# Fourteen pairs of gate tiles instead of twelve, with sums formed during attention, a result parked in DRAM, and low parts of ten weights made by transfers

## The chip, the cores and the metric

The kernel runs on one core of one Trainium2 chip. The metric is the time of one execution on the device in microseconds (us), the median of several runs. A profile is one execution recorded by the hardware profiler; its times are in us from the start of its span.

Engines are called as the profile calls them: PE (TensorE, the matmuls), PEld (PE's weight loads), DVE (VectorE), ACT (ScalarE), POOL (GpSimd), and SP (SyncE, whose queue issues most transfers; POOL's own queue issues the others).

## The reference

One layer of a backbone over 640 tokens (512 of a sample, 128 of a prompt) with 1024 features. An input `h` (a modulated norm of `x`) goes through four mixers, whose outputs are gated, summed, projected and added to `x`; a feed-forward part with a convolution follows. What bears on the change is this part:

```python
proj = h @ w_in                       # split into a_x a_b a_c b_q b_ff b_fb b_i b_g c_q c_k c_v d_u d_v
y_a = a_b * dwconv3(a_c * a_x, conv_a_w, conv_a_b)
y_b = hgrn2_bidir(b_q, b_ff, b_fb, b_i, b_g, ...)
y_c = neighbourhood_attention(c_q, c_k, c_v, ...)     # the prompt: context_attention
y_d = chunk_gmlp(d_u, d_v, ...)
g_a, g_b, g_c, g_d = split(sigmoid(h @ w_gate + b_gate), 4)
merged = g_a * (y_a @ w_br_a) + g_b * (y_b @ w_br_b) + g_c * (y_c @ w_br_c) + g_d * (y_d @ w_br_d)
x = x + g1 * (merged @ w_o)
```

`w_gate` is 1024 x 4096, each `w_br` 256 x 1024, each y 640 x 256.

## The kernel before

**Precision.** Every large product is made of three matmuls on numbers split in two. A weight `raw` (F32) is copied by ScalarE into a high part (F32R), and the low part is `raw - high`, a subtraction on VectorE; `feat` (L356) loads a weight tile and does both, `split_y` (L682) does it for a branch's y, `g_split` (L1058) for an operand of `h`. For some weights of the feed-forward part the low part is made without VectorE: `low_dma` (L1370) has ScalarE write `-high` into the place of the low part, and then POOL's queue sends `raw` there by a transfer that adds (`accum_op=ALU.add`). With `xh` and `xl`, high and low part of `h`, a product is `wh*xh + wh*xl + wl*xh`.

**Tiles.** A tile is 128 output features by 640 tokens, in two halves of 320 (`HC`), so a matmul is 128 x 128 by 320 columns. `gemm` (L392) does 3 matmuls for each of the 8 blocks of 128 input features and each half: 48. A plain gate tile (`gate_tile`, L980) makes these 48 for `h @ w_gate`, takes a sigmoid on ScalarE, makes 12 more for `y @ w_br`, and VectorE multiplies the two and adds them to `merged` (regions MG0, MG1): 60 matmuls.

**Pairs.** Two gate tiles n and n + 4 of one branch are also computed together: input features, output features and tokens cut in halves make a 2 x 2 by 2 x 2 block product, which takes 7 block products instead of 8 (`gprod`, L1128, numbered 1 to 7, of 12 matmuls each). For this, sums of weight blocks are formed for each pair (`g_sums`, `g_b`, `g_c`) and four sums of blocks of `h` once for all (`g_operands`, L1029). With a11, a12, a21, a22 for the blocks of h (first index the half of the features or of the tokens as the code has it): a22 := a21 - a22, a21 := a11 - a21, a11 := a22 - a11, a12 := a12 + a11; the last is operand 3, the others operands 5, 7 and 6. Each is then split into high and low part.

A pair is written out by hand in `g_pair` (L1166): in one call stand the products of pair p, the end of pair p - 1 (its second sigmoid, branch and merge), and the preparation of the weights of pair p + 1. Instructions made through `ovec`, `oact` and `opool` keep their order in the program there. `gp_load` (L1066) loads a pair's two raw weights (10 blocks of 128 x 128 each, 640 KB), one into the rotating pool `raw` (3 buffers), the other into `raw` or region G by turns; the prepared weights go into the pool `w` (3 buffers) for even pairs and into regions C, B, D for odd ones (`gunit`, L1075). The first pair's weights are prepared by `g_first` (L1214) ahead of the last plain gate tiles.

**Order of stages.** A list `units` holds projections in the order of `SECTIONS` (last: ck, cq, cv, ac, ax, ab, two tiles each), then the plain gate tiles, then the pairs. `ahead` loads a unit's weight up to 4 units ahead and prepares it up to 2 ahead. The order of the branches is d, a, b, c (`BR`); before, the eight tiles of branch d are plain and a, b, c are done as 12 pairs (`PAIRS`). Jobs that run beside them are Python generators that are advanced by `tick`, whose argument counts the matmul time issued: `hgrn` gives y_b, `gmlp` y_d, `conva` y_a, `attn` y_c, `ada_cols` the modulation's columns (`w_adt`, loaded into A and H). The order of instructions on each engine's queue thus follows from these yields and from the scheduler, and `drain` advances the jobs until something is done.

**Places.** Regions (A to H, X0, X1, F, MG0, MG1, XH, XL0, XL1, S0) are named pieces of on-chip memory; a new use of a region waits for the last use of the old one. C holds y_c and B attention's operands; E holds the split y_b and D the split y_d; `h` in F32 was written to DRAM at the start (`hdr`). `attn` (L738) has, for each of 16 units, `s1` (scores, exponential), `s2` (normalisation on VectorE, transposes on PE) and `s3` (product with the values). y_c is written to DRAM (`ycd`) after attention and is read back into A by POOL's queue when the last pair of branch b is through (L1180).

The lines that say where the sums stand before:

```python
        if (bi, n) == (0, 0):
            start(g_operands())
    ...
    def g_operands():
        while "yc" not in R:
            yield 1
        nc.sync.dma_start(ycd, R["yc"].bitcast(F32))
        f = [region(t, [P, 2, 4, HC]) for t in "CB"]
```

Of the kernel before, what the change touches and what calls it, by code (L numbers as in the profile page):

```python
# [16 lines left out]
P = 128  # L17
# [3 lines left out]
BRIDGE = 4  # L21
LORD = "w0 1 5 w1 w2 2 6 3 7"
SPL = 0
WARM = [80, 120]
UE = [5, 3]
XP = ()
XE = ()
T = 640
# [22 lines left out]
def tile_step(ctx: ExitStack, tc: tile.TileContext, a: dict, outs: list, dbg=None):  # L51
# [301 lines left out]
        act(w[0], raw, AF.Copy)  # L353
        vec.tensor_tensor(w[1], raw, w[0].bitcast(F32), ALU.subtract)  # L354

    def feat(src, kt=8):  # L356

        raw = rp.tile([P, kt, P], F32, tag="raw", name=nm("raw"))
        nc.sync.dma_start(raw, src)

        def prep(parts=False, tag=None):
            if tag is None:
                w = wp.tile([P, 2, kt, P], F32R, tag="w", name=nm("w"))
            else:
                w = region(tag, [P, 2, kt, P], F32R)
            act(w[:, 0], raw, AF.Copy)  # L366
            low = lambda: vec.tensor_tensor(w[:, 1], raw, w[:, 0].bitcast(F32), ALU.subtract)  # L367
            if parts:
                return w, low
            low()  # L370
            return w
        return prep
# [52 lines left out]
    def evac_in(sec, n, ps):  # L425
        psv = None if isinstance(ps, list) else ps[:, :, 0:HC]
        if sec in ("ff", "fb"):
            d = 0 if sec == "ff" else 1
            ff = need("A", "FF", [P, 2, 2, T])
            kk = need("B", "KK", [P, 2, 2, T])  # L430
            if psv is None:
                for c in range(2):
                    cs = slice(c * HC, (c + 1) * HC)
                    act(ff[:, d, n, cs], ps[c], AF.Sigmoid)
                    act(kk[:, d, n, cs], ps[c], AF.Sigmoid, scale=-1.0)
            else:
                act(c2(ff[:, d, n]), psv, AF.Sigmoid)
                act(c2(kk[:, d, n]), psv, AF.Sigmoid, scale=-1.0)
            i = d * 2 + n
            vec.tensor_scalar(ff[:, d, n], ff[:, d, n], oml[:, i:i + 1], lb[:, i:i + 1],  # L440
                              ALU.mult, ALU.add)
            vec.tensor_scalar(kk[:, d, n], kk[:, d, n], oml[:, i:i + 1], None, ALU.mult)
        elif sec == "q":
            dd = need("D", "HD", [P, 2560])
            act(c2(dd[:, n * T:(n + 1) * T]), psv, AF.Silu)
        elif sec == "g":
            o = need("MG1", "HO", [P, 2560])
            act(c2(o[:, 1280 + n * T:1280 + (n + 1) * T]), psv, AF.Silu)
        elif sec == "du":
            x0 = need("X0", "DX0", [P, 2560])  # L450
            act(c2(x0[:, n * T:(n + 1) * T]), psv, AF.Copy)
        elif sec in ("ac", "ax", "ab"):
            if (sec, n) == ("ac", 0):
                drain(lambda: "hgrn_out" in R)
            y = need("MG0", "YA", [P, 2, 2, T])
            if sec == "ac":
                act(c2(y[:, 0, n]), psv, AF.Copy)
                return
            if sec == "ab":
                drain(lambda: "conv" in R)  # L460
            x = y[:, 0 if sec == "ax" else 1, n]
            vec.tensor_tensor(c2(x), psv, c2(x), ALU.mult)  # L462
            if (sec, n) == ("ab", 1):
                drain(lambda: "ada39" in R)
                R["ya"] = split_y("A", y[:, 1].rearrange("p n t -> p (n t)"))
        elif sec in ("ck", "cq", "cv"):
            if sec == "cv":
                dst = need("G", "CG", [P, 1280])[:, n * T:(n + 1) * T]
            else:
                f = need("F", "CF", [P, 2560])  # L470
                o = 0 if sec == "ck" else 1280
                dst = f[:, o + n * T:o + (n + 1) * T]
            sc = 0.125 if sec == "cq" else 1.0
            cg, cw = (4, 16) if sec == "cq" else (8, 8)
            dv = dst[:, 0:TS].rearrange("p (g r c) -> p r g c", g=cg, r=8)
            for (b, r0, r1) in ((0, 0, 5), (1, 5, 8)):
                src = ps[:, b, 0:(r1 - r0) * 64].rearrange("p (r g c) -> p r g c", g=cg, c=cw)
                act(dv[:, r0:r1], src, AF.Copy, scale=sc)
            act(dst[:, TS:T], ps[:, 1, 192:320], AF.Copy, scale=sc)

    def hgrn():
# [184 lines left out]
        for t in range(5):  # L668
# [6 lines left out]
                vec.scalar_tensor_tensor(s, m[:, pr * P:(pr + 1) * P],  # L675
                                         p1[:, C_HN + pr:C_HN + pr + 1], s, ALU.mult, ALU.mult)
            yield 0.4
        R["yb"] = split_y("E", sg)
        R["hgrn_done"] = True
        R["yd"] = split_y("D", R["yt"])  # L680

    def split_y(tag, y):  # L682
        w = region(tag, [P, 2, 2, T], F32R)
# [54 lines left out]
    def attn():  # L738
# [46 lines left out]
        for pr in range(2):  # L785
            ten.transpose(m[:, pr * P:(pr + 1) * P], cv[:, pr * T + TS:(pr + 1) * T], ident)
            pe(0.11)
        vec.tensor_copy(vpt, m[:, 0:256])
        nc.sync.dma_start(o_cv[0, 0].rearrange("h s d -> s h d"), vpt.rearrange("p (h d) -> p h d", h=4))
        yield 0.4  # L790
        ast = sp.tile([P, 48], F32, tag="ast", name=nm("ast"), bufs=1)
# [106 lines left out]
        for u in range(0, 16, 2):  # L898
            if u < 14:
                s1(u + 2)  # L900
                yield HD[6]
            for i in range(2):
                s2(u + i)
                yield 1.2
            s3(u)
            yield HD[8]
        R["yc"] = yc

    ld, rd = {}, {}
# [8 lines left out]
    def in_tile(sec, n, w):  # L918
        ps = pg()
        gemm(ps, w, 0, 8, xhk, xlk)  # L920
        evac_in(sec, n, ps)
        if n == 1:
            R[sec + "_done"] = True
        if n == 1 and sec in starts:
            start(starts[sec](), 1.5, SLACK[sec])
            if sec == "q":
                start(ada_cols(range(16, 40), "S0", col_home, HD[4]), HD[7])

# [30 lines left out]
    for s in SECTIONS:  # L959
        for n in range(2):  # L960
# [1 line left out]
                plain(lambda s=s, n=n: rows(a["w_tok"][TOK.index(s), n], 4, 256),  # L962
                      lambda w, s=s, n=n: tok_tile(s, n, w))
            else:
                plain(lambda s=s, n=n: feat(a["w_in"][OFF[s] // P + n]),
                      lambda w, s=s, n=n: in_tile(s, n, w))

    hdr = dram.tile([2, P, 4, T], F32, name="hdr")
# [1 line left out]

    BR = ["d", "a", "b", "c"]
    GI = dict(a=0, b=1, c=2, d=3)
    PAIRS = [(bi, n) for bi in range(1, 4) for n in range(4)]
    GPAIR = len(PAIRS)
    ycd = dram.tile([P, 2, 2, T], F32, name="ycd")
    merged = []
    MHT = ["E", "A", "B", "D"]
    mh = []

    def gate_tile(bi, n, w):  # L980
        br = BR[bi]
        if (bi, n) == (0, 0):
            start(g_operands())
        ps = pg()
        gemm(ps, w, 0, 8, xhk, xlk)
        gt = gp.tile([P, T], F32, tag="gt", name=nm("gt"))
# [23 lines left out]
    for bi in range(4):  # L1010
        for n in range(8):
# [2 lines left out]
            br = BR[bi]  # L1014

            def ld_(bi=bi, n=n, br=br):
                return feat(a["w_gate"][GI[br] * 8 + n], 10)

            def cp(w, bi=bi, n=n):
                gate_tile(bi, n, w)  # L1020
# [6 lines left out]
    gx, gw = {}, {}  # L1027

    def g_operands():  # L1029
        while "yc" not in R:  # L1030
            yield 1
        nc.sync.dma_start(ycd, R["yc"].bitcast(F32))
        f = [region(t, [P, 2, 4, HC]) for t in "CB"]
        for c in range(2):
            for h in range(2):
                nc.sync.dma_start(f[c][:, h], hdr[h][:, :, c * HC:(c + 1) * HC])
        yield 8
        (a11, a12), (a21, a22) = [[x[:, h] for h in range(2)] for x in f]
        ops = {i: region(t, [P, 2, 4, HC], F32R) for i, t in ((6, "X0"), (5, "X1"), (7, "F"))}
        gx["x"] = {i: (x[:, 0], x[:, 1]) for i, x in ops.items()}  # L1040
        for i, h, c in ((1, 0, 0), (2, 1, 0), (4, 1, 1), (3, 0, 1)):
            cs = slice(c * HC, (c + 1) * HC)
            gx["x"][i] = xh[:, 4 * h:4 * h + 4, cs], xl[h][:, :, cs]
        gx["t3"] = a12
        vec.tensor_tensor(a22, a21, a22, ALU.subtract)
        yield 1.5
        vec.tensor_tensor(a21, a11, a21, ALU.subtract)
        yield 1.5
        vec.tensor_tensor(a11, a22, a11, ALU.subtract)
        yield 1.5  # L1050
        vec.tensor_tensor(a12, a12, a11, ALU.add)
        yield 1.5
        for i, x in ((6, a11), (5, a22), (7, a21)):
            g_split(i, x)
            yield 1.5
        R["gx"] = True

    def g_split(i, x):  # L1058
# [107 lines left out]
    def g_pair(p_, r):  # L1166
# [902 lines left out]
```

## Time and profile before

| | us |
|---|---|
| median of 3 runs | 1047.86 |
| lowest, highest | 1046.7, 1052.12 |
| the profiled execution's own time | 1051.51 |
| its span, first to last instruction | 1049.7 |
| PE busy | 1030.0 (98%) |
| VectorE busy | 795.3 (76%) |
| ScalarE busy | 518.7 (49%) |
| POOL busy | 95.6 (9%) |
| mean granted clock | 0.993 |

The page gives the span in 40 slices of some 26 us; this is PE, VectorE and the clock, in tenths:

```profile
PE   8999999999999999999999999999999999999997
DVE  6558789789967377677768688998888887695734
PEclk9999999999999999999999999999999999999999
```

In a row of instructions the first numbers are the start and the duration (timeline) or the busy time and the mean duration in ns (groups), then engine, line, operation, `output<-input` with the program's names, sizes, and in brackets the idle time ahead and what ended it. Matmuls overlap: the duration of one is longer than the step from one to the next. In the chain of waits a row is a stretch of the chain that ended last: start, length, engine and line. The releasers are worked out from semaphore events.

### The profile page before, as it was taken

The page shows a single profiled execution, that of the slowest core. Times are in us where ns is not written, and L with a number is a line of the kernel's source. Part 1 is how long each engine was busy: PE and PEld are TensorE (multiplying, and loading weights), DVE is VectorE, ACT ScalarE, POOL GpSimd, SP SyncE. Part 2 cuts the span into 40 slices and gives each one's busy share as a digit, 9 for nine tenths or more (in the row PEclk, how much of TensorE's full clock was granted, in tenths as well). Part 3 has the DMA queues.
Part 4 walks back from the last instruction along what each step waited for, and adds up shares of the span by engine and source line. Part 5 has one row for each costly group of instructions (what it writes and reads, how often), then busy time and mean ns, then how long its engine had stood idle before and what let it go on. Part 6 is the DMA issues. An engine that isn't in the chain of part 4 may idle for free.

```text
span 1049.7 us, 18767 instructions
## 1 busy us (share of the span) xinstructions
PE 1030.0 (98%) x7648; PEld 967.4 (92%) x7648; DVE 795.3 (76%) x1284; ACT 518.7 (49%) x889; POOL 95.6 (9%) x139
## 2 busy tenths in 40 slices
PE   8999999999999999999999999999999999999997
PEld 6799989999889999999998889999999998888886
DVE  6558789789967377677768688998888887695734
ACT  6252343333243345444445377777677775632532
POOL 1000010202100000000000011221111121000201
PEclk9999999999999999999999999999999999999999
DMA  9663433454234131431258475666665559974212
GB/s 372 238 246 119 135 96 119 125 177 150 70 117 148 53 117 55 147 99 55 89 203 319 159 256 132 171 162 163 162 161 152 146 151 262 340 264 161 81 41 101
DMA packets 52855, 165.67 MB, mean 158 GB/s; under 512 B 7808, under 2 KB 14880, under 8 KB 49696
## 3 DMA queue, kind: packets, MB, share of 16 engines
q1 hardware_dynamic: 42992, 137.19, 38.3%
q0 software_dynamic: 9776, 27.28, 11.1%
q8 instruction: 60, 0.98, 0.4%
q14 instruction: 27, 0.22, 0.1%
HBM read 131.52 MB, written 21.52 MB: 146 GB/s over the span
## 4 chain that ended last, share of the span: by engine, by line
PE 92%; DVE 2%; DMA 2%; issue 2%; ACT 1%; POOL 0%; SPq 0%; POOLq 0%; ACTq 0%; DVEq 0%
PE g L1476 19%; PE g L401 19%; PE m L1135 14%; PE g L1789 8%; PE m L1789 6%; PE m L1476 5%; PE g L1148 4%; PE m L1271 3%; PE g L947 2%; PE g L1271 2%; PE g L1891 1%; PE m L562 1%; PE m L211 1%; PE m L887 1%; DMA E<-actd 1%
## 5 line engine op out<-in xcount | busy, mean ns | idle before, releaser
L401 PE MATMUL g<-XH,w 128*128 128x320 f32 x832 | 201.2, 318 | 0.2 <-DVE MG L462 0.2
L401 PEld LDWEIGHTS g<-XH,w 128*128 128x128 f32 x832 | 143.1, 189 | 2.8 <-issue 2.0
L401 PE MATMUL g<-XL,w 128*128 128x320 f32 x416 | 129.6, 311 | 0.0
L401 PEld LDWEIGHTS g<-XL,w 128*128 128x128 f32 x416 | 78.9, 190 | 0.8 <-issue 0.5
L354 DVE TENSOR_TENSOR w<-raw,w 128x1024 fp32r<-128x1024 f32 x34 | 41.5, 1221 | 16.1 <-ACT w L353 15.3
L1789 PE MATMUL g<-w,XH 128*128 128x512 f32 (+1 forms) x216 | 47.5, 372 | 0.0
L353 ACT ACTIVATE w<-raw 128x1024 fp32r<-128x1024 f32 x34 | 35.8, 1053 | 19.1 <-PE g L1271 9.8
L1789 PEld LDWEIGHTS g<-w,XH 128*128 128x128 f32 x216 | 38.5, 188 | 7.3 <-DVE X L131 0.2
L1135 PE MATMUL m<-XH,w 128*128 128x320 f32 x192 | 45.0, 309 | 0.0
L366 ACT ACTIVATE w<-raw 128x1024 fp32r<-128x1024 f32 (+1 forms) x29 | 32.5, 1121 | 23.3 <-PE g L401 7.5
L367 DVE TENSOR_TENSOR w<-raw,w 128x1024 fp32r<-128x1024 f32 (+1 forms) x29 | 37.5, 1294 | 5.7 <-ACT w L366 5.5
L131 DVE SCALAR_TENSOR_TENSOR X<-MG,p2t,X 128x641 f32<-128x641 f32 x44 | 38.9, 884 | 2.2 <-ACT X L131 1.4
L1789 PE MATMUL m<-w,XH 128*128 128x512 f32 (+1 forms) x180 | 40.3, 369 | 0.0
L1789 PE MATMUL g<-w,XL 128*128 128x512 f32 (+1 forms) x180 | 40.1, 373 | 0.0
L131 DVE SCALAR_TENSOR_TENSOR X<-X,p2t,X 128x641 f32<-128x641 f32 x44 | 38.9, 884 | 1.2 <-ACT X L131 0.3
L1476 PE MATMUL g<-XL,C 128*128 128x320 f32 x240 | 38.6, 310 | 0.4 <-ACT MG L131 0.4
L1476 PE MATMUL g<-XL,w 128*128 128x320 f32 x240 | 38.7, 310 | 0.0
L1789 PEld LDWEIGHTS g<-w,XL 128*128 128x128 f32 x180 | 32.2, 188 | 6.8 <-DVE dt L1800 0.6
L1476 PEld LDWEIGHTS g<-XL,C 128*128 128x128 f32 x240 | 35.9, 188 | 1.1 <-ACT MG L131 1.1
L1476 PEld LDWEIGHTS g<-XL,w 128*128 128x128 f32 x240 | 35.9, 188 | 0.7 <-ACT MG L131 0.3
L1789 PEld LDWEIGHTS m<-w,XH 128*128 128x128 f32 x180 | 31.3, 189 | 5.3
L1789 PE MATMUL m<-w,XL 128*128 128x512 f32 (+1 forms) x150 | 33.2, 368 | 0.0
(544 smaller groups left out, 2703.9 us busy)
## 6 DMA issues: line engine op xcount, KB each, us to landing
raw<-in_w_up_dram SPq DMA_DIRECT2D x31, 512.0 KB, 5.1
raw<-in_w_gp_dram SPq DMA_DIRECT2D x18, 640.0 KB, 4.0
raw<-in_w_in_dram SPq DMA_DIRECT2D x22, 512.0 KB, 4.4
raw<-in_w_down_dram SPq DMA_DIRECT2D x22, 512.0 KB, 4.0
H<-in_w_adt_dram SPq DMA_DIRECT2D x16, 512.0 KB, 4.3
actd<-X POOLq DMA_DIRECT2D x22, 320.5 KB, 5.5
G<-in_w_up_dram SPq DMA_DIRECT2D x11, 512.0 KB, 4.7
X<-in_w_adt_dram SPq DMA_DIRECT2D x10, 512.0 KB, 3.7
```

Of the source, the lines that this page charges most:

```text
L131: r = f(*args, **kw)
L353: act(w[0], raw, AF.Copy)
L354: vec.tensor_tensor(w[1], raw, w[0].bitcast(F32), ALU.subtract)
L366: act(w[:, 0], raw, AF.Copy)
L367: low = lambda: vec.tensor_tensor(w[:, 1], raw, w[:, 0].bitcast(F32), ALU.subtract)
L401: mm(o, w[:, h, k0 + k, :], r(k)[:, s], start=(k == 0 and i == 0), stop=(k == kt - 1 and i == 2))
L947: mm(o, x(kx)[:, ts], w[:, h, k, :], start=(kx == 0 and i == 0), stop=(kx == 7 and i == 2))
L1135: mm(o, w[:, k, :], x[:, k, :], start=(first and k == 0 and j == 0), stop=(k == 3 and j == 2), skip_group_check=True)
L1148: mm(pb[:, c, 0:HC], w[:, h + k, :], y[:, x, k, s], start=(k == 0 and j == 0), stop=(k == 1 and j == 2))
L1271: mm(m, mh[k // 2][:, hx, k % 2, t * P:(t + 1) * P], wo[q][:, hw, k % 2, :], start=(k == 0 and i == 0), stop=(k == 7 and i == 2))
L1476: mm(o, w[:, k, :], x[:, k, :], start=(first and k == 0 and j == 0), stop=(k == 3 and j == 2), skip_group_check=True)
L1789: mm(acc[nh][t + c0 // 256][:, 0:c1 - c0], sl[k][hx][:, t * P:(t + 1) * P], w[:, hw, k, c0:c1], start=(kk_ == 0 and k == 0 and i == 0), st ...
```

## The change

- Two of the four pairs of branch d, (0,2) and (0,3), are done as pairs too: 14 pairs, and four plain gate tiles (n = 0, 1, 4, 5). `merged` of these is begun by `g_merge`.
- `g_operands` starts when the projection cv is through. Once attention has taken its copies of cv (`R["cg"]`) it loads three pieces of h from `hdr`, two into D and one into G, and makes three of the four sums as soon as y_a is there. It splits operand 7 into F when the last scores are done (`R["scores"]`), and operands 5 and 6 into X1 and X0 when attention is over. Then the fourth piece of h is loaded into D; it is added in the first pair.
- y_b is split into D and written to DRAM (`ybd`), so that D is free, and is read back into E by POOL's queue after pair (0,3). y_d is split into E.
- The weights of ac, ax, ab and of the four plain gate tiles, ten in all, get their low part by `low_dma`.
- `g_operands` holds G, so the first pair's second raw weight goes into the rotating pool and G is used for odd pairs. Odd pairs use the regions in the order B, C, D.
- The write of y_c to `ycd` moves to the end of `attn`.

```diff
+NPL = 2
+LOWD = ("ac", "ax", "ab", "d")
...
-    def feat(src, kt=8):
+    def feat(src, kt=8, dma=False):
...
             act(w[:, 0], raw, AF.Copy)
+            if dma:
+                low_dma(w[:, 1].rearrange("p a b -> p (a b)"), raw.rearrange("p a b -> p (a b)"))
+                return w
...
+    ybd, ycd = [dram.tile([P, 2, 2, T], F32, name=n) for n in ("ybd", "ycd")]
...
-        R["yb"] = split_y("E", sg)
+        nc.sync.dma_start(ybd, split_y("D", sg).bitcast(F32))
         R["hgrn_done"] = True
-        R["yd"] = split_y("D", R["yt"])
+        R["yd"] = split_y("E", R["yt"])
...
         vec.tensor_copy(vpt, m[:, 0:256])
+        R["cg"] = True
...
+            if u == 14:
+                R["scores"] = True
...
+        nc.sync.dma_start(ycd, yc.bitcast(F32))
         R["yc"] = yc
...
             start(starts[sec](), 1.5, SLACK[sec])
+            if sec == "cv":
+                start(g_operands())
...
-    PAIRS = [(bi, n) for bi in range(1, 4) for n in range(4)]
+    PAIRS = [(0, n) for n in range(NPL, 4)] + [(bi, n) for bi in range(1, 4) for n in range(4)]
...
-        if (bi, n) == (0, 0):
-            start(g_operands())
...
-                return feat(a["w_gate"][GI[br] * 8 + n], 10)
+                return feat(a["w_gate"][GI[br] * 8 + n], 10, br in LOWD)
...
     def g_operands():
-        while "yc" not in R:
+        while "cg" not in R:
             yield 1
-        nc.sync.dma_start(ycd, R["yc"].bitcast(F32))
-        f = [region(t, [P, 2, 4, HC]) for t in "CB"]
-        for c in range(2):
-            for h in range(2):
-                nc.sync.dma_start(f[c][:, h], hdr[h][:, :, c * HC:(c + 1) * HC])
-        yield 8
-        (a11, a12), (a21, a22) = [[x[:, h] for h in range(2)] for x in f]
-        ops = {i: region(t, [P, 2, 4, HC], F32R) for i, t in ((6, "X0"), (5, "X1"), (7, "F"))}
-        gx["x"] = {i: (x[:, 0], x[:, 1]) for i, x in ops.items()}
+        d, g = region("D", [P, 2, 4, HC]), region("G", [P, 4, HC])
+        part = lambda h, c: hdr[h][:, :, c * HC:(c + 1) * HC]
+        for x, h, c in ((d[:, 0], 0, 1), (d[:, 1], 1, 1), (g, 0, 0)):
+            nc.sync.dma_start(x, part(h, c))
+        while "ya" not in R:
+            yield 1
+        a21, a22, a11 = d[:, 0], d[:, 1], g
+        vec.tensor_tensor(a22, a21, a22, ALU.subtract)
+        yield 2
+        vec.tensor_tensor(a21, a11, a21, ALU.subtract)
+        yield 2
+        vec.tensor_tensor(a11, a22, a11, ALU.subtract)
+        gx["x"] = {}
         for i, h, c in ((1, 0, 0), (2, 1, 0), (4, 1, 1), (3, 0, 1)):
             cs = slice(c * HC, (c + 1) * HC)
             gx["x"][i] = xh[:, 4 * h:4 * h + 4, cs], xl[h][:, :, cs]
-        gx["t3"] = a12
...
-        for i, x in ((6, a11), (5, a22), (7, a21)):
+        for i, x, t, key in ((7, a21, "F", "scores"), (5, a22, "X1", "yc"), (6, a11, "X0", "yc")):
+            while key not in R:
+                yield 1
+            y = region(t, [P, 2, 4, HC], F32R)
+            gx["x"][i] = y[:, 0], y[:, 1]
             g_split(i, x)
             yield 1.5
+        nc.sync.dma_start(a22, part(1, 0))
+        gx["t3"] = a22, a11
         R["gx"] = True
...
-        r.append(region("G", [P, 10, P]) if p_ % 2 == 0 else rp.tile([P, 10, P], F32, tag="raw", name=nm("raw")))
+        r.append(region("G", [P, 10, P]) if p_ % 2 else rp.tile([P, 10, P], F32, tag="raw", name=nm("raw")))
...
-        return region("CBD"[i], [P, 5, 4, P], F32R)
+        return region("BCD"[i], [P, 5, 4, P], F32R)
...
-        ovec.tensor_tensor(c2(gt), pb, c2(gt), ALU.mult)
         mg = merged[n // 4][:, n % 4, :]
+        ovec.tensor_tensor(c2(gt if bi else mg), pb, c2(gt), ALU.mult)
+        if not bi:
+            return
         ovec.tensor_tensor(mg, mg, gt, ALU.add)
...
-            if PAIRS[q] == (1, 3):
-                R["yc"] = region("A", [P, 2, 2, T], F32R)
-                pool.dma_start(R["yc"], ycd)
+            if PAIRS[q] in ((0, 3), (1, 3)):
+                n_, t, y = ("yb", "E", ybd) if PAIRS[q][0] == 0 else ("yc", "A", ycd)
+                R[n_] = region(t, [P, 2, 2, T], F32R)
+                pool.dma_start(R[n_], y)
...
+        if q < 0:
+            t3, x6 = gx["t3"]
+            ovec.tensor_tensor(t3, t3, x6, ALU.add)
         if nx:
             g_a(n, r[n])
         gprod(b3, p_, 2, q < 0)
         if q < 0:
-            g_split(3, gx["t3"])
+            g_split(3, gx["t3"][0])
...
     def g_first(r):
+        drain(lambda: "ada39" in R)
         g_a(0, r[0])
```

More of the change, by code (lines that the diff above doesn't have):

```diff
@@ L964, in tile_step @@
             else:
-                plain(lambda s=s, n=n: feat(a["w_in"][OFF[s] // P + n]),
+                plain(lambda s=s, n=n: feat(a["w_in"][OFF[s] // P + n], dma=s in LOWD),
                       lambda w, s=s, n=n: in_tile(s, n, w))
@@ L972, in tile_step @@
     GI = dict(a=0, b=1, c=2, d=3)
-    PAIRS = [(bi, n) for bi in range(1, 4) for n in range(4)]
+    PAIRS = [(0, n) for n in range(NPL, 4)] + [(bi, n) for bi in range(1, 4) for n in range(4)]
     GPAIR = len(PAIRS)
-    ycd = dram.tile([P, 2, 2, T], F32, name="ycd")
     merged = []
@@ L1043, in g_operands @@
             gx["x"][i] = xh[:, 4 * h:4 * h + 4, cs], xl[h][:, :, cs]
-        gx["t3"] = a12
[L1045 to L1052, printed above, removed]
-        for i, x in ((6, a11), (5, a22), (7, a21)):
+        for i, x, t, key in ((7, a21, "F", "scores"), (5, a22, "X1", "yc"), (6, a11, "X0", "yc")):
[3 more added lines that the diff above has]
+            gx["x"][i] = y[:, 0], y[:, 1]
             g_split(i, x)
             yield 1.5
+        nc.sync.dma_start(a22, part(1, 0))
+        gx["t3"] = a22, a11
         R["gx"] = True
```

## The prediction

> **What bounds the kernel now.** I began with the page's spans and engine shares, then asked who TensorE (PE) waited for, and then how busy each engine is in the stages that the change touches: 207 to 307 us (attention beside the projections and the first gate tiles), 307 to 363 (the other gate tiles), and one pair (363 to 379).
>
> ```profile
> span 1049.7 us, 18767 instructions
> PE 1030.0 (98%) x7648; PEld 967.4 (92%) x7648; DVE 795.3 (76%) x1284; ACT 518.7 (49%) x889; POOL 95.6 (9%) x139
> ```
> ```profile
> PE g L1891 <- ACT XH L1853: 2.6, 2, 1.5
> ...
> PE g L401 <- DVE MG L462: 0.2, 1, 0.2
> ```
> ```profile
> 207.00:307.00 100.00, 99.62 (x715) 89.76 (x714) 86.63 (x180) 35.37 (x75) 12.41 (x16) 1.00 0.35 112
> 307.00:363.00 56.00, 56.00 (x384) 56.00 (x383) 27.05 (x26) 19.77 (x21) 0.00 (x0) 1.00 0.38 130
> 363.00:379.00 16.00, 16.00 (x111) 16.00 (x110) 12.75 (x20) 7.78 (x15) 0.00 (x0) 1.00 0.36 124
> ```
> The columns after the stretch and its length are PE, weight load, VectorE (DVE), ScalarE (ACT) and POOL busy, the granted clock, DMA share and GB/s. PE is busy 98% of the span, and from 207 to 379 it lacks 0.38 us. The longest wait, 2.6 us in two parts, lies in the opening; here the only one listed is 0.2 us. The clock is 1.00. So this part ends when PE has worked off its matmuls: only fewer matmuls shorten it, and each new wait of PE lengthens it by its full size. VectorE, 87% busy until 307, is the engine nearest behind.
>
> **What the change removes.** A pair takes 7 products of 12 matmuls and two branches of 12, 108; two plain tiles take 2 x 60 = 120. Two more pairs save 24 matmuls of 320 columns.
>
> ```profile
> 352.17 1.92 PE L401 MATMUL g<-D,w 128*128 128x320 f32 x12
> 353.93 0.31 PE L401 MATMUL g<-XH,w 128*128 128x320 f32 x1
> ```
> ```profile
> 306.53 56.37 PE g L401 x383
> 362.89 8.80 PE m L1135 x60
> ```
> The first fence is PE's timeline, the second the chain of waits. The single matmul of 0.31 us overlaps its neighbours: twelve take 353.93 - 352.17 = 1.76 us, 0.147 each. The chain says the same of a plain tile (56.37 / 383 = 0.147) and of a product (8.80 / 60 = 0.147). So the gain is 24 x 0.147 = **3.5 us** and no more; multiplying by 0.31 would give twice that.
>
> Ten weights lose their subtraction on VectorE and get a negated copy on ScalarE and an accumulating transfer from POOL's queue.
>
> ```profile
> L367 DVE TENSOR_TENSOR w<-raw,w 128x1024 fp32r<-128x1024 f32 (+1 forms) x10 | 13.2, 1324 | 0.5 <-ACT w L366 0.4
> ```
> ```profile
> 318.10 1.49 DVE L1045 TENSOR_TENSOR B<-B 128x1280 f32<-128x1280 f32 x1 [5.17 <-DMA B<-hdr]
> ```
> VectorE loses 13.2 us before 307 and gets there three sums of h and one low part of a sum, 4 x 1.49 = 6.0, and some 2 us of the first pair's weights: about 5 us less. ScalarE gets ten copies of about 1.2 us, 11.6, on 35.37 busy of 100. As sums of busy time these cost PE nothing, being hidden under the 99.62 us of matmuls. What can cost is the order in each queue, which I took from the two compiled programs.
>
> **Transfers moved.** The second branch's y goes to DRAM before three pieces of h may be loaded into the same place, so the sync queue waits for that write, and behind it stand a projection weight and a modulation column load.
>
> ```profile
> 219.44 1.49 DVE L686 TENSOR_TENSOR E<-MG,E 128x1280 fp32r<-128x1280 f32 x1 [1.34 <-ACT E L685]
> ```
> ```profile
> 231.31 0.35 SPq L244 DMA_DIRECT2D A<-in_w_adt_dram  x1
> ```
> ```profile
> raw<-in_w_gp_dram SPq DMA_DIRECT2D x18, 640.0 KB, 4.0
> G<-in_w_gp_dram SPq DMA_DIRECT2D x6, 640.0 KB, 3.9
> C<-raw POOLq DMA_DIRECT2D x10, 256.0 KB, 4.1
> ycd<-C SPq DMA_DIRECT2D x1, 1280.0 KB, 9.0
> B<-X POOLq DMA_DIRECT2D x1, 384.0 KB, 6.3
> ```
> y is split by 220.9; a write of this size landed after 9.0 us; 229.9 is ahead of 231.3, when the column load was issued anyway. Cost 0. The reloads of y by POOL (the third branch's was there before) are asked for a pair and more ahead of use: 0.
>
> **Attention's first transposes.** The changed program places them 13 matmuls (1.9 us) earlier in PE's order, with a sum of h (1.49) put ahead of their operand on VectorE and a subtraction (1.2) gone.
>
> ```profile
> 243.45 0.41 DVE L867 TENSOR_SCALAR X<-X,ast 128x384 f32<-128x384 f32 x1
> ```
> ```profile
> 244.73 0.49 PE L870 MATMUL m<-cst,X 128*128 128x128 f32 x3
> ```
> Here the operand was ready 0.9 us before PE came. PE now comes at 242.8 and finds it at 243.9 + 0.3 or a little later: a wait of 1.4 to 1.6 us if nothing gives. Later in attention VectorE has less to do, and PE gets part of it back; bounds 0 and 1.6, I take **0.4**, nearer the lower end because VectorE's load falls.
>
> **The first gate tile's sigmoid.** This is where I expect the main cost. The first pair's second raw weight is now loaded into a rotating buffer whose last user is the third gate weight, and that is free only when the weight's low-part transfer has landed. ScalarE's order then holds a copy of this raw weight *ahead* of attention's last exponentials and the first gate tile's sigmoid; the second tile's matmuls need the sigmoid's PSUM bank.
>
> ```profile
> 276.84 1.27 ACT L366 ACTIVATE w<-raw 128x1280 fp32r<-128x1280 f32 x1 [1.05 <-PE g L401]
> ...
> 284.10 1.27 ACT L685 ACTIVATE A<-MG 128x1280 fp32r<-128x1280 f32 x1
> ...
> 291.31 0.62 ACT L860 ACTIVATE X<-X,ast 128x384 f32<-128x384 f32 x1 [2.00 <-DVE ast L859]
> 291.84 0.19 ACT L860 ACTIVATION_READ_ACCUMULATOR X<-X,ast 128x1 f32 x1
> ...
> 292.64 1.28 ACT L988 ACT_TABLE_LOAD   x1
> 293.94 0.79 ACT L988 ACTIVATE gt<-g,p1t 128x640 f32<-128x640 f32 x1
> ...
> 366.28 0.41 ACT L131 ACTIVATE H<-raw 128x256 fp32r<-128x256 f32 x1
> ```
> The negated copy follows the split of the first branch's y: 284.10 + 1.27 + 1.27 = 286.6. The transfer of 640 KB has no row. Below it lies the 256 KB one, 4.1 us; above, the strided 384 KB one's rate, 6.3 x 640 / 384 = 10.5. I take 5.5, nearer the 256 KB row, because that is the same unstrided form, and loads show little growth with size (640 KB land in 4.0). Then the sync queue loads (4.0): 296.1. Then the copy 0.41, two exponentials 2 x 0.81, table 1.28, sigmoid 0.79: 300.2.
>
> PE would be there at: start of the pairs 362.7 (the chain), less seven tiles of 60 (420 x 0.147 = 61.6), less the attention work that the new order leaves for later.
>
> ```profile
> 295.10 0.80 PE m L887 x10
> 296.74 0.48 PE m L870 x3
> ```
> That is two value products and two transposes, 2 x 0.80 + 2 x 0.48 = 2.6: 298.5. The wait is 300.2 - 298.5, about **1.7 us**; with 4.1 it is 0.3, with 10.5 it is 6.7. Behind the blocked copy stand those exponentials, and VectorE waits for their sums with the copies that feed the value products. At its end two exponential table loads fewer are needed, since the sigmoid no longer falls between exponentials; hidden either way.
>
> The Trainium skill (DMA: Bandwidth & Descriptors, Anatomy of one DMA, SWDGE path) fits a transfer from GpSimd as 2.0 us plus bytes over 436 GB/s. By that an estimate for 640 KB is 3.5 us, the wait disappears and the whole sum is 1.4 us better, but it also gives 2.6 for 256 KB, where the row says 4.1; the row decides.
>
> **Start of the pairs.** One buffer holds a sum of h until the pair's own addition, so the second pair's second raw is loaded after it, no longer ahead.
>
> ```profile
> 364.87 0.68 DVE L131 TENSOR_TENSOR w<-G,w 128x512 fp32r<-128x512 f32 x1
> ...
> 369.04 0.69 DVE L131 TENSOR_TENSOR S<-S,raw 128x512 f32<-128x512 f32 x1
> ```
> ```profile
> 369.77 1.58 ACT L131 ACTIVATE B<-S 128x1024 fp32r<-128x1024 f32 x2 [0.44 <-DVE S L131]
> 371.73 0.44 ACT L131 ACTIVATE gb<-m 128x320 f32<-128x320 f32 x1 [0.39 <-PE m L1135]
> ```
> From the pair's start: the last low part ends at 365.55 - 362.73 = 2.8, the addition 1.49 makes 4.3, the load 3.9 makes 8.2, two sums and a low part 1.8 make 10.0, the two copies 1.58 and the accumulator's copy 0.44 some 12.4, with a short wait for the third sum. PE's new order puts 84 matmuls, 12.3 us, ahead of the product that needs this copy. Cost 0.1 to 1.4 (if the load takes 1.2 us more); I take **0.3**, as its rows land in 3.9 to 4.0. The sums' own splits end soon after attention (307), the first use is past 325: no cost.
>
> **Sum.** -3.5 + 0.4 + 1.7 + 0.3 = -1.1 us on the profiled run, whose span of 1049.7 lies in a run of 1051.51 us; that run is 3.65 above the median, so I apply the difference to the median: 1047.86 - 1.1 = **1046.8 us**.
>
> **The rivals.**
>
> *The full gain.* If the transfers land like the 256 KB row and VectorE's relief removes the wait at the transposes, -3.5 + 0.3 + 0.1 = -3.1: 1044.8. For it: VectorE's smaller load, and transfers started well ahead. Against: ScalarE's order, in which a wait for DMA stands before the sigmoid.
>
> *Slower, by the ScalarE queue.* One mechanism: the low-part transfer of 640 KB holds the raw buffer, ScalarE stands at the copy, and PE at the second tile. At the upper bound it gives 6.7, with the other upper bounds -3.5 + 1.6 + 6.7 + 1.4 = +6.2: 1054.1. It turns the sum positive once the transfer takes more than 6.6 us, and passes half a per cent near 10. For it: the 384 KB row at 6.3. Against: all 256 KB rows.
>
> A rule of the Trainium skill (SBUF - State Buffer, Who interferes with whom) speaks for it: VectorE in a two-port mode locks GpSimd out, and its descriptors wait. The 4.1 us above were measured beside a busy VectorE, so no long lock shows there.
>
> *The change does not do what it says:* the pairs would start before the sums are ready and the saved matmuls become waiting, about 1048. The margin of some 18 us between 307 and 325 speaks against it.
>
> **Chances.** The forecast 0.48, the full gain 0.27, slower by the queue 0.20, the last 0.05. Half a per cent, 5.2 us, is about what a measurement of this kernel can tell from no change. Faster by more than that needs more than all the matmuls removed and is left to effects not listed: 0.07. Slower by more takes the queue's upper half and mishaps beyond it: 0.16. The rest, 0.77, is within. Range: from 1047.86 - 3.5 with 0.6 for the scatter, 1043.8, to 1053.8, just under the sum of the upper bounds.
>
> **What would show it.** PE's count of 320-column matmuls down by 24, at 0.147 each. In the attention stage PE idle in front of the second gate tile with ScalarE's sigmoid as releaser, and ScalarE idle for DMA before the copy of the first pair's raw weight. The first pair without a wait above 0.5 us. The landing time of the 640 KB transfers decides: near 4 the full gain, above 7 slower. A wait of PE in any other place, or late projection weights, would prove the forecast wrong.

## The result, and the profile after

| | before | after |
|---|---|---|
| median of 20 runs each, us | 1048.05 | 1053.36 |
| lowest, highest | 1044.44, 1056.62 | 1049.26, 1059.27 |
| ratio, 95% interval | | 1.0052 [1.0039, 1.0066] |
| the profiled execution, its span | 1051.51, 1049.7 | 1057.19, 1055.4 |

The change costs some 5.4 us. The forecast was 1046.8, a gain of 1.1 us: the time lies in the upper end of the stated range, but it moved the other way. First, the waits of PE in the changed kernel (total us, times, longest):

```profile
PE m L879 <- DVE X L876: 6.7, 1, 6.7
PE g L1910 <- ACT XH L1872: 2.6, 2, 1.5
PE g L1808 <- DVE dt L1819: 2.4, 1, 2.4
...
PE m L1147 <- ACT gb L133: 1.0, 1, 1.0
```

The first is new: L879 holds attention's transposes, L876 the normalisation of the scores. The one at L1808 is in the last stage, hundreds of us behind the change: VectorE stands there for a row read back from DRAM, 9.02 us against 6.00 in the kernel before. PE's wait there is 1.2 to 2.4 us in every run below that has both fourteen pairs and low-part transfers, and at most 0.2 us in the others; why was not followed. The last is the second pair's. Windows of the stretch show the price (the columns as before; the granted clock and the DMA share stand ahead of GB/s):

```profile
207.00:250.00 43.00, 36.27 (x262) 34.44 (x261) 28.06 (x60) 18.07 (x36) 10.03 (x11) 0.95 0.84 239
...
218.00:243.00 25.00, 24.58 (x182) 23.08 (x180) 14.71 (x27) 14.04 (x27) 3.17 (x4) 1.00 0.99 290
243.00:250.00 7.00, 0.68 (x4) 0.71 (x5) 5.93 (x17) 1.31 (x4) 2.21 (x3) 0.70 0.49 157
250.00:256.00 6.00, 6.00 (x36) 4.97 (x36) 3.98 (x8) 0.28 (x1) 0.00 (x0) 0.78 0.87 238
```

The same 25 us in the kernel before:

```profile
218.00:243.00 25.00, 25.00 (x185) 23.59 (x184) 21.83 (x41) 12.44 (x28) 2.87 (x4) 1.00 0.48 148
```

The DMA engines went from 48% to 99% busy, while VectorE went from 21.8 to 14.7 us: it had less to do and stood waiting. PE's clock fell behind the stall, 0.70 and 0.78 on average: 7 x 0.30 + 6 x 0.22 = 3.4 us' worth of clock, or 6.8 us at half rate, of which PE was at work for the 3.3 us or so from 249.3 on. So the stall cost 6.7 us and some 1.7 us more. The Trainium skill (TensorE: Matmul & The Clock Gate, Part 1: The HAM clock gate) says that an idle window of about 3.4 us halves the clock; the trace agrees, with two such windows. Shorter waits were followed by half a clock too: in `e5_loads_late` below, PE waits 2.25 us until 303.85, and from 304.3 on the clock is at half for 3.4 us.

What came late is seen on the sync queue of the changed kernel (SPq rows are issues) and on its VectorE:

```profile
220.92 0.33 SPq L686 DMA_DIRECT2D ybd<-D  x1
223.98 0.58 SPq L1046 DMA_DIRECT2D G<-hdr  x1
...
230.77 1.70 SPq L1046 DMA_DIRECT2D D<-hdr  x2
232.57 1.58 SPq L361 DMA_DIRECT2D raw<-in_w_in_dram  x1
234.24 0.93 SPq L246 DMA_DIRECT2D A<-in_w_adt_dram  x1
```
```profile
241.68 1.49 DVE L1050 TENSOR_TENSOR D<-D 128x1280 f32<-128x1280 f32 x1 [5.18 <-DMA D<-hdr]
244.24 1.23 DVE L257 SCALAR_TENSOR_TENSOR junk<-A,S 128x1024 bf16<-128x1024 f32 x1 [1.07 <-DMA A<-in_w_adt_dram]
...
248.76 0.74 DVE L876 TENSOR_SCALAR X<-X,ast 128x384 f32<-128x384 f32 x2
```

VectorE works in order. It stood 5.18 us in front of the first sum of h, whose pieces had not landed, then 1.07 us in front of a modulation column, asked for at 234.24 and there at 244.2: 10.0 us, where the same load took 3.4 before. It was also asked for 3 us later than before: the sync queue stood 3.3 us until the write of y had landed (220.92 + 9.8 = 230.7), and the two loads into D and a weight's load were issued ahead of it. Behind these two stood the scores' maxima, so ScalarE's exponentials and the normalisation came late as well.

### The profile page after: what moved, and what is told of

It reads as the page before. It is cut to its first block, busy times and chain, and to the rows that moved or that the text cites. A ratio compares the mean times of both kernels' runs of the same rounds, so it can differ in the third digit from the quotient of the medians.

```text
span 1055.4 us, 18799 instructions
## 1 busy us (share of the span) xinstructions
PE 1026.9 (97%) x7624; PEld 962.8 (91%) x7624; DVE 793.8 (75%) x1296; ACT 532.3 (50%) x915; POOL 107.4 (10%) x150
## 4 chain that ended last, share of the span: by engine, by line
PE 89%; DMA 4%; DVE 3%; ACT 2%; issue 1%; POOL 0%; SPq 0%; POOLq 0%; ACTq 0%; DVEq 0%
PE g L1495 19%; PE m L1147 15%; PE g L406 15%; PE g L1808 8%; PE m L1808 6%; PE m L1495 5%; PE g L1160 5%; PE m L1290 3%; PE g L961 2%; PE g L1290 2%; PE g L1910 1%; PE m L570 1%; PE m L213 1%; DMA A<-in_w_adt_dram 1%; DMA S<-growd 1%
## 5 line engine op out<-in xcount | busy, mean ns | idle before, releaser
L406 PE MATMUL g<-XH,w 128*128 128x320 f32 x704 | 173.4, 320 | 0.0
L406 PEld LDWEIGHTS g<-XH,w 128*128 128x128 f32 x704 | 122.4, 191 | 2.8 <-issue 1.4
L406 PE MATMUL g<-XL,w 128*128 128x320 f32 x352 | 110.2, 313 | 0.0
L406 PEld LDWEIGHTS g<-XL,w 128*128 128x128 f32 x352 | 67.3, 191 | 0.3 <-issue 0.2
L1147 PE MATMUL m<-XH,w 128*128 128x320 f32 x224 | 52.6, 309 | 1.0 <-ACT gb L133 1.0
L1808 PE MATMUL g<-w,XH 128*128 128x512 f32 (+1 forms) x216 | 47.4, 372 | 0.0
L1808 PEld LDWEIGHTS g<-w,XH 128*128 128x128 f32 x216 | 38.5, 188 | 7.2 <-DVE X L133 0.2
L1808 PE MATMUL g<-w,XL 128*128 128x512 f32 (+1 forms) x180 | 41.3, 381 | 2.4 <-DVE dt L1819 2.4
L1808 PEld LDWEIGHTS g<-w,XL 128*128 128x128 f32 x180 | 32.9, 192 | 9.6 <-DVE dt L1819 3.1
L1808 PE MATMUL m<-w,XH 128*128 128x512 f32 (+1 forms) x180 | 40.8, 371 | 0.0
L1147 PEld LDWEIGHTS m<-XH,w 128*128 128x128 f32 x224 | 38.3, 188 | 1.3 <-ACT gb L133 1.3
L1495 PE MATMUL g<-XL,w 128*128 128x320 f32 x240 | 38.8, 310 | 0.0
L368 ACT ACTIVATE w<-raw 128x1024 fp32r<-128x1024 f32 (+1 forms) x25 | 27.4, 1095 | 20.5 <-PE g L406 6.9
L1808 PEld LDWEIGHTS m<-w,XH 128*128 128x128 f32 x180 | 31.7, 191 | 5.6
L1495 PEld LDWEIGHTS g<-XL,w 128*128 128x128 f32 x240 | 35.9, 188 | 0.7 <-ACT MG L133 0.3
L133 ACT ACTIVATE w<-raw 128x1024 fp32r<-128x1024 f32 (+3 forms) x40 | 34.7, 884 | 1.0 <-PE g L406 1.0
```

Source lines behind the costliest of these rows:

```text
L133: r = f(*args, **kw)
L406: mm(o, w[:, h, k0 + k, :], r(k)[:, s], start=(k == 0 and i == 0), stop=(k == kt - 1 and i == 2))
L1147: mm(o, w[:, k, :], x[:, k, :], start=(first and k == 0 and j == 0), stop=(k == 3 and j == 2), skip_group_check=True)
L1495: mm(o, w[:, k, :], x[:, k, :], start=(first and k == 0 and j == 0), stop=(k == 3 and j == 2), skip_group_check=True)
L1808: mm(acc[nh][t + c0 // 256][:, 0:c1 - c0], sl[k][hx][:, t * P:(t + 1) * P], w[:, hw, k, c0:c1], start=(kk_ == 0 and k == 0 and i == 0), st ...
```

## The experiments

Three causes could make that wait. A: the low-part transfers fill the DMA engines, so loads land late. B: the write of y, and the loads of h that wait for it, stand ahead of the column load on the sync queue. C: the sum stands ahead of the normalisation on VectorE. Each run below is timed in 5 rounds against the kernel before. The code that is the same in all of them took different times in single executions (from the start to a matmul near 200 us 195.9 to 202.3 us), so for where the time goes I compare a stretch: the time from that matmul to the pairs' first product. To it are added the 35.2 us of four plain tiles where these have become pairs, and the 163.2 us of the kernel before are taken off. All is worked out from start times in the traces. The changed kernel has +7.1 there. The fixed windows, such as 218 to 243, do not follow this shift of up to some 6 us.

**No low-part transfers** (`e1_low_on_vector`)

```diff
-LOWD = ("ac", "ax", "ab", "d")
+LOWD = ()
```

> The changed kernel, but with all ten low parts formed by VectorE again (no low-part transfers); in the order that results, the three sums of h also stand late on VectorE, behind most of attention. Write of y, loads of h and the column load behind them on the sync queue stay as in the changed kernel. Theory A (the low-part transfers fill the DMA engines, so that the column load lands late and VectorE, in order, stands): the column load behind the loads of h lands in 4 to 5 us instead of 10, PE's wait of 6.7 us at attention's transposes is gone, and the time is that of before less 3.5 and plus about 1 at the second pair, ratio about 0.998. Theory B (the sync queue's wait for the write of y, and the loads of h ahead of the column load, are enough): the load is still asked for 3 us later than before and shares its time with 1.25 MB of h, PE still waits 3 us or more, ratio 1.001 or above. Theory C (the sum's place on VectorE ahead of attention's normalisation): the wait is gone as under A; this run alone can't tell A from C.

Ratio 0.9988 [0.9971, 1.0005], stretch +1.3. The column load:

```profile
229.75 0.53 SPq L246 DMA_DIRECT2D A<-in_w_adt_dram  x1
```
```profile
237.37 1.23 DVE L257 SCALAR_TENSOR_TENSOR junk<-A,S 128x1024 bf16<-128x1024 f32 x1 [1.01 <-DMA A<-in_w_adt_dram]
```

It was asked for no later than before (231.31 there; counted from the matmul near 200 us the two agree to 0.1 us), though the write and the loads of h were ahead of it. The write landed after 5.5 us here, against 9.8 in the changed kernel, and the queue did not stand for it. So by themselves the write and the loads of h do not make the issue late, and that part of B falls. Landing took 7.6 us, more than the 4 to 5 that A allowed: the loads of h do slow it. But only 1.0 us of VectorE was lost and PE lost 0.6 us in two waits. The DMA engines were at 0.75 from 218 to 243.

**Transfers for the gate weights alone** (`e2_low_gates_only`)

```diff
-LOWD = ("ac", "ax", "ab", "d")
+LOWD = ("d",)
```

> Low-part transfers for the four gate weights alone; the six weights of ac, ax, ab have theirs formed by VectorE. The sums of h stand late on VectorE. Theory A: as without any transfers, since those of the projections are the ones beside the loads of h; no wait of 6.7 us, ratio about 0.998, and with the gate tiles' transfers back the wait that I forecast at the first gate tile's sigmoid (1.7 us, 0.3 to 6.7) can show, ratio up to 1.000. Theory B: PE waits 3 us or more at attention's transposes, ratio 1.001 or above. Theory C: no wait there.

Ratio 0.9979 [0.9959, 0.9999], stretch 0.0; the column load landed after 6.9 us and PE waited 0.4 us at the transposes. It is the six transfers of the projections that hurt, those that run beside the loads of h. The first gate tile's sigmoid held nobody.

**The sums held in place** (`e3_sums_in_place`)

```diff
-        vec.tensor_tensor(a22, a21, a22, ALU.subtract)
+        pin = tc.keep_in_program_order
+        pin(vec.tensor_tensor(a22, a21, a22, ALU.subtract))
...
-        vec.tensor_tensor(a21, a11, a21, ALU.subtract)
+        pin(vec.tensor_tensor(a21, a11, a21, ALU.subtract))
...
-        vec.tensor_tensor(a11, a22, a11, ALU.subtract)
+        pin(vec.tensor_tensor(a11, a22, a11, ALU.subtract))
```

> The changed kernel with the three sums of h held at their place in the program, so that none stands ahead of attention's first normalisations on VectorE; all ten low-part transfers, the write of y and the loads of h stay where they are. Theory C (the sum, which waits for its load, holds VectorE): the wait of 6.7 us falls below 1 us, ratio about 0.998. Theories A and B (the column load is late): VectorE's next instruction in order, the modulation column, waits for a load that still lands 10 us after its issue, PE's wait stays at 5 to 7 us, ratio 1.003 to 1.005.

Ratio 1.0058 [1.0039, 1.0078], stretch +6.8. PE's longest wait, the issue of the column load, and VectorE's wait for it:

```profile
PE m L879 <- DVE ast L875: 6.9, 1, 6.9
```
```profile
230.87 0.58 SPq L246 DMA_DIRECT2D A<-in_w_adt_dram  x1
```
```profile
241.80 1.22 DVE L257 SCALAR_TENSOR_TENSOR junk<-A,S 128x1024 bf16<-128x1024 f32 x1 [6.30 <-DMA A<-in_w_adt_dram]
```

C falls as the cause. With the sum out of the way VectorE simply stood at the next thing whose load was late, for 6.30 us. The load was asked for at 230.87, which is 1.5 us later than before when counted from the matmul near 200 us, and was there after 10.9 us. In the changed kernel the sum had only taken over this wait.

**The loads of h late as well** (`e5_loads_late`): as the run before, and

```diff
-        for x, h, c in ((d[:, 0], 0, 1), (d[:, 1], 1, 1), (g, 0, 0)):
-            nc.sync.dma_start(x, part(h, c))
         while "ya" not in R:
             yield 1
+        for x, h, c in ((d[:, 0], 0, 1), (d[:, 1], 1, 1), (g, 0, 0)):
+            tc.keep_in_program_order(nc.sync.dma_start(x, part(h, c)))
```

> As the run with the sums held in place, and the three loads of h held at their place too, behind the gate weights' loads: the column load then waits neither for the write of y nor behind the loads of h. The ten low-part transfers stay. Theory B: the column load is issued as early as before, PE's wait is gone, ratio about 0.998 (0.3 us or more lost if the sums are late for the pairs). Theory A: the write of y and two 512 KB low-part transfers still share the DMA engines with it, so it lands in 6 us or more; PE waits 1 to 4 us, ratio 1.000 to 1.003. Theory C: no wait, as in the run before.

Ratio 1.0001 [0.9980, 1.0021], stretch +2.9. The column load landed after 5.8 us and cost VectorE 0.86 us, with all ten transfers and the write of y there. So A alone does not do it either. The time was lost at another place, as the expectation for B had in brackets, but dearer: the loads of h, issued at 289, held the sums, and these held the last normalisation.

```profile
298.25 1.49 DVE L1051 TENSOR_TENSOR D<-D 128x1280 f32<-128x1280 f32 x1 [2.30 <-DMA D<-hdr]
```
```profile
303.85 0.55 PE L879 MATMUL m<-cst,X 128*128 128x128 f32 x3 [2.25 <-DVE X L876]
```

**The fourth sum early**, once with the gate weights' transfers (`e6_gates_only_sum_early`), once without any (`e6_vector_sum_early`); beside `LOWD`:

```diff
         gx["t3"] = a22, a11
+        yield 6
+        vec.tensor_tensor(a22, a22, a11, ALU.add)
...
-        if q < 0:
-            t3, x6 = gx["t3"]
-            ovec.tensor_tensor(t3, t3, x6, ALU.add)
```

> Low-part transfers for the four gate weights alone, and the fourth sum of h (a12 + a11) formed by VectorE ahead of the pairs instead of within the first pair, so that region G is free and the second pair's second raw weight can be loaded earlier. If the 1.0 us that PE waits for ScalarE's copy at the second pair comes from this load, the wait goes: with the 0.4 us left at attention's transposes -3.5 + 0.4 = -3.1 us, ratio about 0.997. Rival: the sum, which waits for its piece of h, holds VectorE ahead of the first pair's weights, as the sum in attention did in the changed kernel; then the first pair starts late by 1 to 3 us, ratio 0.998 to 1.000.

> The same early fourth sum, with no low-part transfers at all. VectorE has 13 us more to do before the pairs than with ten transfers. If VectorE's load isn't what holds PE there, -3.5 and the waits of about 1.2 us that the run without transfers had at the attention and the sigmoid, 0.9978; if the fuller VectorE makes the sum late, 1.000.

0.9975 [0.9957, 0.9994] and 0.9968 [0.9953, 0.9983]. The wait at the second pair is gone in both: from the first pair's start to the output projection 221.8 us, where it was 223.1 to 223.5 in the runs before. The sum held nothing. Whether the gate weights' transfers are worth anything can't be told from these two.

**The low parts alone, in the kernel before** (`e7_low_parts_alone`, `e9_projections_alone`, `e9_gates_alone`): `feat` with its `dma` argument as in the change, twelve pairs, no loads of h in attention; the ten weights, then the six of ac, ax, ab, then the four gate weights.

> The kernel before, with nothing changed but ten low parts (ac, ax, ab and four gate weights) made by transfers; no loads of h during attention, no write of y, twelve pairs. Theory that only both together, transfers and loads of h, make the column load late: it lands in 4 to 7 us, PE waits below 2 us at attention's transposes, ratio 0.999 to 1.002. Theory A in its strict form (the transfers alone fill the DMA engines): it lands in 8 us or more, PE waits 4 us or more, ratio 1.004 or above.

> The kernel before, with the low parts of the six weights of ac, ax and ab alone made by transfers. The run with ten transfers in the kernel before gained 2.4 us between the projections and the pairs, though PE waits there only 0.4 us by the profile. If that gain comes from VectorE's relief during the first half of attention (207 to 250 us), these six carry it: 2 us or more, ratio 0.997 to 0.998. If it comes from the gate weights' part, or from something outside this stretch, ratio 0.999 to 1.001.

> The kernel before, with the low parts of the four gate weights alone made by transfers. If the six weights of the projections carry the gain, nothing changes here, ratio 0.999 to 1.001, and PE's matmuls in attention stand as they did before; if the gate weights do, 0.997 to 0.998.

0.9969 [0.9954, 0.9985], 0.9970 [0.9953, 0.9986] and 0.9971 [0.9954, 0.9989]. A in its strict form falls: in the first the column load landed after 4.5 us and nobody waited for it. And the transfers are a gain by themselves, which I had costed at nothing. The three runs over 207 to 307 us, all ten, six, four; then the kernel before:

```profile
207.00:307.00 100.00, 100.00 (x737) 91.52 (x736) 77.26 (x170) 43.92 (x83) 20.84 (x25) 1.00 0.60 159
```
```profile
207.00:307.00 100.00, 100.00 (x733) 91.52 (x732) 79.63 (x174) 41.30 (x82) 21.52 (x23) 1.00 0.53 149
```
```profile
207.00:307.00 100.00, 99.64 (x725) 90.74 (x724) 82.14 (x176) 41.09 (x80) 12.50 (x16) 1.00 0.45 137
```
```profile
207.00:307.00 100.00, 99.62 (x715) 89.76 (x714) 86.63 (x180) 35.37 (x75) 12.41 (x16) 1.00 0.35 112
```

PE is as good as fully busy in all, yet gets through 737 matmuls instead of 715. With the windows begun at the same matmul the counts are 734, 730 and 722, and 713 before. The stretch gives -2.4, -2.6 and -0.8 us for the same 1157 matmuls. Start times show where: attention's own 208 small matmuls (scores, transposes, value products) take 19.9, 21.3 and 22.2 us, each counted to the next start, against 23.5 before; the 900 of the projections and gate tiles take 138.9, 137.3 and 138.1, against 137.7. So the six weights carry what this stretch gains. The expectation that the four would then change nothing failed: their ratio is some 2 us better than their stretch explains, though its interval reaches down to a gain of 1.1 us. What the rest is, and why six and four do not add up, stays open.

**Both, apart from each other** (`e8_loads_mid_attention`, `e8_loads_end_attention`): all ten transfers, the sums held in place and the fourth early as above, and the loads of h held at a later point in attention:

```diff
-        while "cg" not in R:
+        while "hload" not in R:
             yield 1
...
+            tc.keep_in_program_order(nc.sync.dma_start(x, part(h, c)))
...
+            if u == 4:
+                R["hload"] = True
```

(`u == 8` in the second.)

> Fourteen pairs with all ten low parts by transfers. The three loads of h are issued in the middle of attention (behind its third round of scores), the three sums are held at their place behind y_a, the fourth sum is formed ahead of the pairs. If the wait of 6.7 us came only from the loads of h and the low-part transfers meeting between 220 and 245 us, and if the late sums in the run with late loads only suffered from their loads being late, no wait above 1 us is left in attention; the gains then add: -3.5 for the matmuls and the 2.4 us that the low parts alone gained in attention in the kernel before, -5.9 us, ratio 0.994 to 0.995. Rival: the loads of h meet the low-part transfers again between 255 and 270 us and hold the columns there; a wait of 1 to 4 us, ratio 0.997 to 1.001.

> The same with the loads of h issued later still, behind the fifth round of scores and ahead of the first pair's weights. If the loads' place within the attention doesn't matter as long as they miss the write of y and land ahead of the sums, the ratio is as in the run beside it, 0.994 to 0.995; if the sums must wait for them, VectorE stands ahead of the last normalisations, 1 to 3 us, 0.996 to 0.998.

0.9952 [0.9936, 0.9968] and 0.9956 [0.9940, 0.9972], medians 1042.81 and 1043.79 us: faster than both kernels. The sum of the two gains had been 5.9 us; 4.6 to 5.0 came by the ratios. Stretch -2.7 and -2.6, and no wait of PE in attention above 0.2 us. The column load landed after 4.5 us in the first; its issue, that of the loads of h, and the first sum:

```profile
228.76 0.39 SPq L246 DMA_DIRECT2D A<-in_w_adt_dram  x1
...
251.12 2.34 SPq L1048 DMA_DIRECT2D D<-hdr  x2
253.55 1.58 SPq L1048 DMA_DIRECT2D G<-hdr  x1
```
```profile
284.12 1.48 DVE L1053 TENSOR_TENSOR D<-D 128x1280 f32<-128x1280 f32 x1
```

Here too the loads met low-part transfers, but the sums come 30 us later and nothing waits for them.

## Why the prediction failed

**Transfers moved, costed at 0: this is the step that failed.** The write of y landed after 9.8 us (9.0 taken), yet the column load was asked for 3 us later than before: the time that the loads ahead of it take to issue, 230.77 to 234.24, was not in the sum. Without the low-part transfers (`e1_low_on_vector`) it was asked for no later. The larger part that it left out is how long the load then takes: of the 9.5 us by which the column came late (244.2 against 234.7), 6.6 are a longer landing, 10.0 instead of 3.4. I compared times of issue, and never added up what the DMA engines had to carry between 218 and 243 us: 1.25 MB of y, 1.9 MB of h, and the accumulating transfers beside the usual weights. The runs show that the stall takes both the early loads of h and the six transfers (the write of y is in all six):

| | loads of h early | transfers of ac, ax, ab | DMA share 218 to 243 | column load, us | PE's longest wait there, us | ratio |
|---|---|---|---|---|---|---|
| changed kernel | yes | yes | 0.99 | 10.0 | 6.7 | 1.0052 |
| `e3_sums_in_place` | yes | yes | 0.98 | 10.9 | 6.9 | 1.0058 |
| `e1_low_on_vector` | yes | no | 0.75 | 7.6 | 0.4 | 0.9988 |
| `e2_low_gates_only` | yes | no | 0.79 | 6.9 | 0.4 | 0.9979 |
| `e5_loads_late` | no | yes | 0.86 | 5.8 | 2.2, of late sums | 1.0001 |
| `e8_loads_mid_attention` | no | yes | 0.82 | 4.5 | 0.2 | 0.9952 |

Up to 7.6 us is nearly covered; 10 us is a stall. The Trainium skill (DMA: Bandwidth & Descriptors, Issuing engines are not separate DMA queues) says that transfers of every issuing engine share the same 16 DMA engines; the table agrees: transfers of POOL's queue slow loads of the sync queue.

**The matmuls removed: right.** PE has 7648 - 7624 = 24 fewer, and the fourteen pairs of the early-sum runs took 221.8 / 14 = 15.84 us each, 108 x 0.147.

**Attention's first transposes: right place, wrong size.** I gave them 0.4 us with a bound of 1.6, from the work put ahead of the operand. That work's own load was late, so the bound was none. The 1.7 us that the clock added behind the wait had no term in the sum.

**The first gate tile's sigmoid: 1.7 us forecast, not seen.** The parts were there: the 640 KB transfer took 5.2 us (5.5 taken), the load 3.9, and the copy stood ahead of the exponentials and the sigmoid in the changed kernel. But PE was some 8 us late by then and did not wait at the sigmoid. Small waits there, 0.2 to 0.6 us, show in other runs, the largest in `e1_low_on_vector`, which has no such transfer. In the fastest runs the scheduler put the sigmoid ahead of that copy. What it would cost in the changed order with PE on time was not tried.

**Start of the pairs: 0.3 forecast, 1.0 measured**, within its bounds (0.1 to 1.4). The chain of waits names the reason, a load that took 5.51 us instead of 3.9, behind the sum that freed its place; with the sum moved ahead (the two early-sum runs) the wait was gone.

```profile
337.35 1.41 DVE D L133
...
338.78 5.51 DMA G<-in_w_gp_dram
```

**VectorE's relief, costed at nothing: wrong too, the other way.** It was "hidden under the 99.62 us of matmuls", since "only fewer matmuls shorten" this part. The low parts alone gained about 2.5 us in this stretch, with PE busy in both kernels and the same matmuls. Whether the relief itself or the order that came with it gave this is not shown.

**The sum as measured:** -3.5 + 6.7 + 1.7 + 1.0 = +5.9. From the matmul near 200 us to the output projection the changed kernel lost 4.8 in its profiled execution, and by the medians 5.3 as a whole. Some 1.9 us were won back at attention's end (by start times of the same matmul 8.8 us late near 301 us, 6.9 near 310), more than the difference between 5.9 and 4.8. The rival "slower, by the ScalarE queue" gave 1054.1, close to the time, but the mechanism was another: VectorE in front of a late load, not ScalarE. So it was luck that the time fell within the range, whose upper part stood for the ScalarE queue.

**Two slips in the working.** With 3.5 us for the 640 KB transfer the wait of 1.7 us disappears, so the sum is better by 1.7 us, not 1.4. And with the other terms as taken, the sum passes half a per cent at a transfer of 11.8 us; only with the other upper bounds is it near 10. Neither bears on the failure.

## What to carry to other kernels

When a change adds transfers, add up the bytes in flight in each stretch beside the share the DMA engines already have there, and ask which small load behind them an in-order engine stands in front of; a time of issue that has not moved says nothing of the landing. A scheduler's order can put a sum whose load is late in front of urgent work. Holding the sums in place alone gained nothing here; with their loads issued past the crowded 25 us, yet well ahead of the sums, the stall was gone. A busy PE is no proof that relieving another engine is worth nothing: time the same matmuls in both kernels.

## What was not expected of the hardware

- The stall cost a quarter more than its length: 6.8 us at half the clock behind a wait of 6.7 us.
- PE counted as busy 99.6% of a stretch still let some 20 matmuls in 715 go (715 against 737 in 100 us, 713 against 734 from the same matmul on). They were gained in the steps between attention's small matmuls; whether by VectorE's shorter queue or by PE's other order was not separated.
- Loads of one size, 512 KB, landed after 3.4 us in one kernel and 10.9 in another, with the same instruction, asked for within 1.5 us of the same point.
